# Second product of both MLPs: all four sums of weight parts of the last quarter's granules come from DRAM

## Chip, cores and metric

The kernel runs on one core of one Trainium2 chip. The metric is the device time of one execution in microseconds (us); beside it stands one execution taken by the hardware profiler, with a record of every instruction.

## What is computed

The reference runs two transformer blocks on a sequence of 512 tokens with 1024 channels, in float32. Each ends in an MLP with 4096 hidden channels; the rest (mixers, attention, norms) is not touched by the change.

```python
def squared_relu_mlp(h, w1, w2):
    return jnp.square(jax.nn.relu(h @ w1)) @ w2
# first block
x = x + squared_relu_mlp(rmsnorm(x, norm_ffn[l]), ffn_w1[l], ffn_w2[l])
# second block
u = rmsnorm_2(x, norm_mlp_g[i]) @ w_up[i]
x = x + jnp.square(jax.nn.relu(u)) @ w_down[i]
```

## The kernel before

**Number format.** To keep float32 accuracy, every operand is split into a high part (a rounding copy on ACT, `nc.scalar.copy`) and a low part (a subtraction on DVE), and a product is three matmuls: high by high, high by low, low by high (`mm3`, L275 to L277).

**The MLP.** `ffn` (from L967) runs over four quarters `q` of the hidden channels. In each, four granules of the first product (`proj_fm`, weights by `wgran`) give 1024 hidden channels, which are squared and laid down as the operand of the second product (`st_fill`). Then four granules of the second product (`st_gemm`) add 256 output channels each into the residual `x`. Granules of the second product are counted 4q + g, 0 to 15. In the last quarter (granules 12 to 15) `post` runs behind each granule: it starts the norm of the next stage on the two finished tiles of `x` (`norm_tile` in the second MLP, `ev` of `between` in the first), with work on ACT (L307, L314, L317) and on DVE (L308, L318).

**The second product** is cut into two by two blocks in Strassen's manner (Winograd's variant), with seven products instead of eight. Of each granule's weights the four blocks a11, a12, a21, a22 lie in DRAM, 256 KB each. The products need a11, a12, a22 and four sums: s1 = a21 + a22, s2 = a11 + s1, s3 = a11 + a21, s4 = a12 + s2. `st_gemm` runs the products in the order a11, a12, s2, s1, s3, s4, a22, twelve matmuls each, into three PSUM banks X, Y, Z. Behind each one a DVE addition (L947) adds the bank to `x`; X and Z then go on accumulating, so the next product into the same bank waits for that addition.

**Where the sums come from.** s1 and s2 are made in DRAM, in the scratch tile `sums`, by transfers alone: a copy of a block (issued on ACT's queue, L218) and an accumulating transfer on top (on POOL's queue, L222). `sum_jobs` (L208) writes a list of such jobs for both MLPs: for each granule copy a21, add a22 (that is s1), copy a11, add s1 (that is s2), staggered so that an add comes after its copy has had time. `job` takes `rate` jobs off the list each time it is called: in `wgran` (where `wx` is None), in `ffn` behind each granule of the first product, and in `st_gemm`. The rate is 1, but 2 from L514 to the start of the first MLP. `st_weights` (from L892) takes further jobs if the sums of its granule are not made yet (`made`). The copies are ordered behind the last weight cast of `wload` on ACT.

**Loading.** `st_weights` loads A = (a11, a12), B = (a21, s2) and C = (s1, a22) from DRAM on SP's queue (L911) into raw buffers, splits them (L304 on ACT, L305 on DVE), and makes s3 and s4 itself: one DVE addition A + B in place (L924, 128 partitions by 1024), then a split of the result. Raw buffers, and pairs of high and low buffers, go round in rings of five (`wtiles`), in two pools, "wr"/"wh"/"wl" and "wrx"/"whx"/"wlx".

**Order.** The framework lays down the order on each engine when the kernel is built, by the order in the program and its own estimate of what is ready; on the chip each engine works through its queue in that order.

Of the kernel before, what the change touches and what calls it, by code (L numbers as in the profile page):

```python
# [9 lines left out]
F32 = mybir.dt.float32  # L10
# [8 lines left out]
P = 128  # L19
KT = 8  # L20
T = 512
# [44 lines left out]
class Kern:  # L66
    def __init__(self, tc, ctx, D, out, dbg=None):
        self.tc, self.nc, self.ctx, self.D, self.out = tc, tc.nc, ctx, D, out
        self.dbg = dbg or {}
        self.const = ctx.enter_context(tc.tile_pool(name="const", bufs=1))  # L70
        self.wp = ctx.enter_context(tc.tile_pool(name="wp", bufs=3))
        self.wx, self.wn = None, 0
        self.perm = list(range(13))
        self.dp = ctx.enter_context(tc.tile_pool(name="dr", bufs=1, space=DRAM))
        self.sums = {n: [self.dp.tile([P, 2, T], F32, tag=f"{n}{g}", name=f"sums_{n}_{g}") for g in range(16)]
                     for n in ("ffn_w2", "w_down_2")}
        self.jobs, self.made, self.rate, self.rn = [], {}, 1, 0
        self.sp = ctx.enter_context(tc.tile_pool(name="sp", bufs=1))
        self.tp = ctx.enter_context(tc.tile_pool(name="tp", bufs=2))
        self.pd = ctx.enter_context(tc.tile_pool(name="pd", bufs=3, space=PSUM))  # L80
        self.ps = ctx.enter_context(tc.tile_pool(name="ps", bufs=1, space=PSUM))
        self.n = 0
# [20 lines left out]
    def psc(self, tag, bufs=None):  # L103
        return self.pc.tile([P, T], F32, tag=tag, name=self.uid(tag), bufs=bufs)
# [103 lines left out]
    def sum_jobs(self, name):  # L208


        nc, n = self.nc, 16
        W, S = self.D[name], self.sums[name]
        self.made[name] = 0

        def copy(i, j, k):
            if 0 <= i < n:
                with self.tc.issue_after(self.last_cast.ins):
                    nc.scalar.dma_start(S[i][:, j:j + 1], W[i][:, k:k + 1])  # L218

        def add(i, j, src):  # L220
            if 0 <= i < n:
                nc.gpsimd.dma_start(S[i][:, j:j + 1], src(i), accum_op=ALU.add)  # L222
                self.made[name] += j

        for i in range(n + 2):
            self.jobs += [lambda i=i: copy(i, 0, 2), lambda i=i: add(i - 1, 0, lambda g: W[g][:, 3:4]),
                          lambda i=i: copy(i, 1, 0), lambda i=i: add(i - 2, 1, lambda g: S[g][:, 0:1])]

    def job(self):
        for _ in range(self.rate):  # L230
# [327 lines left out]
    def dn_head(self, h, q, k, v, pr, gate, yb_h, yb_l):  # L558
# [125 lines left out]
        for b in range(NB):  # L684
            nc.tensor.matmul(psA[64:128, b * P:b * P + 64], M[0:64, b, 64:128], Tt[0:64, b, 0:64], start=True, stop=True)
        A = b4("dA" + e, 1)
        nc.scalar.copy(A[64:128, :, 0:64], v4(psA)[64:128, :, 0:64])
        psV = psc()
        for b in range(NB):
            nc.tensor.matmul(psV[0:64, b * P:b * P + 64], A[64:128, b, 0:64], Vt[64:128, b, 64:128], start=True, stop=True)  # L690
        TT(out=Vt[0:64, :, 64:128], in0=Vt[0:64, :, 64:128], in1=v4(psV)[0:64, :, 0:64], op=ALU.subtract)
# [200 lines left out]
    def st_weights(self, name, g):  # L892

        nc = self.nc
        while self.made[name] <= g:
            self.jobs.pop(0)()
        a, s = self.D[name][g], self.sums[name][g]
        out = []

        def parts_of(raw):  # L900
            rn = self.rn
            _, hi, lo = self.wtiles(2, T)
            self.rn = rn
            return raw, hi(), lo()

        def load(*srcs):
            raw, hi, lo = (f() for f in self.wtiles(2, T))
            j = 0
            for src in srcs:
                m = src.shape[1]  # L910
                nc.sync.dma_start(raw[:, j:j + m], src)  # L911
                j += m
            return raw, hi, lo

        def split(raw, hi, lo, c=slice(0, 2)):
            self.split_sb(hi[:, c], lo[:, c], raw[:, c])
            return [(hi[:, i], lo[:, i]) for i in range(c.start, c.stop)]

        A = load(a[:, 0:2])
        a11, a12 = split(*A)  # L920
        B = load(a[:, 2:3], s[:, 1:2])
        s2, = split(*B, slice(1, 2))
        C = load(s[:, 0:1], a[:, 3:4])
        nc.vector.tensor_tensor(out=A[0], in0=A[0], in1=B[0], op=ALU.add)  # L924
        s1, a22 = split(*C)
        s3, s4 = split(*parts_of(A[0]))
        return a11, a12, s2, s1, s3, s4, a22
# [512 lines left out]
def body(tc, D, out, dbg=None):  # L1440
    with ExitStack() as ctx:
        K = Kern(tc, ctx, D, out, dbg)
        K.setup()
        mem = K.mixer()
        with tc.tile_pool(name="sp2", bufs=1) as K.sp2:
            op = K.w_out1()
            op = K.xattn(*op, mem)
        K.rate = 1
        with tc.tile_pool(name="fp", bufs=1) as K.fp:
            K.sp2 = K.wx = K.fp  # L1450
            ev, fin = K.between()
            K.ffn("ffn_w1", "ffn_w2", *op, (0, 1, 4, 7, 8, 9, 10), ev)
            K.wx = None
            op2 = fin()
        K.perm = [2, 3, 5, 6, 0, 1, 4, 7, 8]
        mh, ml = K.mixer2(*op2)
        K.perm = list(range(13))
        xh, xl = K.pair((0, 1)), K.pair((4, 7))
        acc = K.new_acc()

        def ev(o, ps):
            K.nc.vector.scalar_tensor_tensor(out=K.x[:, o], in0=ps, scalar=0.5, in1=K.x[:, o], op0=ALU.mult, op1=ALU.add)
            K.norm_tile(o, xh, xl, acc, "norm_mlp_g_2")

        for g in range(4):
            K.proj_fm(K.wgran("w_out_2", g), mh, ml, (2 * g, 2 * g + 1), ev)
        K.dump("x5", K.x)
        with tc.tile_pool(name="fp", bufs=1) as K.fp:
            K.sp2 = K.wx = K.fp
            ev, ple = K.tail()  # L1470
            K.ffn("w_up_2", "w_down_2", xh, xl, acc, (2, 3, 5, 6, 8, 9, 10), ev)
            ple()
# [81 lines left out]
```

## Time and profile before

| | |
|---|---|
| time, median of 3 runs | 1712.49 us (1706.7 to 1714.46) |
| the profiled execution's own time | 1707.82 us |
| its span in the trace | 1706.0 us |
| PE, busy | 1681.1 us (99%) |
| DVE, busy | 1216.6 us (71%) |
| ACT, busy | 822.0 us (48%) |
| POOL, busy | 66.3 us (4%) |
| granted TensorE clock, mean | 0.996 of full |

PE is TensorE's matmul row, PEld its weight loads (which overlap), DVE VectorE, ACT ScalarE, POOL GpSimd; SP issues the loads. A name with q (ACTq, SPq) is an engine's queue, where transfers are issued. Matmuls are pipelined: one takes 0.28 us and the next starts 0.12 us after it. "L924" is line 924 of the kernel. Behind an arrow stands what ended a wait.

### The profile page before, as it was taken

Reading aid. Unit: us, or ns where it says so; the run is one execution under the profiler, and the core shown is the slowest. Engines: PE = TensorE matmul, PEld = TensorE weight load, DVE = VectorE, ACT = ScalarE, POOL = GpSimd, SP = SyncE. Lnnn points to the kernel's source line nnn. Section 1 sums busy time; section 2 is a strip of 40 time slices with the busy share of each in tenths; the row PEclk is TensorE's granted clock in tenths of the full one; section 3 lists DMA queues with packets and bytes.
Section 4 is the critical chain, followed back from the end, with each engine's and each line's share of the span. In section 5 each row is a group of like instructions: output and inputs, shape, how many; then the busy total and the mean of one; then the engine's idle time right before and its main releaser. Section 6 shows DMA issues by size and latency. Waiting matters only on the chain.

```text
span 1706.0 us, 25979 instructions
## 1 busy us (share of the span) xinstructions
PE 1681.1 (99%) x9924; PEld 1456.4 (85%) x9924; DVE 1216.6 (71%) x2574; ACT 822.0 (48%) x1462; POOL 66.3 (4%) x86
## 2 busy tenths in 40 slices
PE   9999999999999999999999999999999999999998
PEld 8988898877898989888988887788888989898987
DVE  6988885756686868688845569865556767676875
ACT  5355654544444444454444457654244444444553
POOL 0200001000000000000000000000000000000000
PEclk9999999999999999999999999999999999999999
DMA  6321357436546464423333332334464454643331
GB/s 202 100 75 53 104 162 182 112 93 171 122 134 165 131 167 131 130 93 107 100 91 101 99 87 68 93 87 118 116 188 128 132 166 131 166 131 123 100 111 50
DMA packets 81948, 205.64 MB, mean 121 GB/s; under 512 B 13088, under 2 KB 14240, under 8 KB 81824
## 3 DMA queue, kind: packets, MB, share of 16 engines
q1 hardware_dynamic: 62672, 169.29, 31.9%
q0 software_dynamic: 9216, 16.78, 6.9%
q10 hardware_dynamic: 9936, 17.91, 3.8%
q8 instruction: 78, 1.28, 0.3%
q14 instruction: 46, 0.38, 0.1%
HBM read 201.59 MB, written 35.65 MB: 139 GB/s over the span
## 4 chain that ended last, share of the span: by engine, by line
PE 88%; DVE 7%; ACT 2%; issue 1%; DMA 1%; SPq 0%; ACTq 0%; DVEq 0%
PE psd L276 21%; PE psd L275 21%; PE psd L277 21%; PE x L275 5%; PE x L276 5%; PE x L277 5%; DVE wl L257 1%; PE c L578 1%; PE c L631 1%; PE lg L1308 1%; PE po L1335 1%; ACT wh L256 1%; DVE acc L318 1%; DVE S L418 1%; PE m L1229 1%
## 5 line engine op out<-in xcount | busy, mean ns | idle before, releaser
L277 PE MATMUL psd<-S,wl 128*128 128x512 f32 (+1 forms) x1256 | 485.1, 387 | 0.6 <-DVE wl L257 0.5
L275 PE MATMUL psd<-S,wh 128*128 128x512 f32 (+1 forms) x1256 | 484.3, 386 | 0.8 <-ACT S L307 0.8
L276 PE MATMUL psd<-S,wh 128*128 128x512 f32 (+1 forms) x1192 | 459.6, 386 | 0.2
L275 PEld LDWEIGHTS psd<-S,wh 128*128 128x128 f32 x1256 | 237.2, 189 | 46.2 <-ACT S L307 1.0
L277 PEld LDWEIGHTS psd<-S,wl 128*128 128x128 f32 x1256 | 237.2, 189 | 45.8 <-DVE wl L257 1.4
L257 DVE TENSOR_TENSOR wl<-wr,wh 128x1024 fp32r<-128x1024 f32 (+2 forms) x160 | 192.0, 1200 | 107.6 <-ACT wh L256 107.0
L276 PEld LDWEIGHTS psd<-S,wh 128*128 128x128 f32 x1192 | 225.0, 189 | 43.4 <-DVE S L305 1.4
L256 ACT CAST wh<-wr 128x1024 fp32r<-128x1024 f32 (+2 forms) x160 | 164.0, 1026 | 160.3 <-PE psd L276 112.3
L276 PE MATMUL psd<-wl,S 128*128 128x256 f32 (+2 forms) x480 | 135.6, 283 | 0.3 <-DVE wl L257 0.3
L275 PE MATMUL psd<-wh,S 128*128 128x256 f32 (+2 forms) x480 | 135.5, 283 | 0.0
L277 PE MATMUL psd<-wh,S 128*128 128x256 f32 (+2 forms) x480 | 135.2, 282 | 0.0
L275 PE MATMUL x<-S,wh 128*128 128x256 f32 x452 | 128.0, 285 | 3.1 <-DVE x_fm L947 2.9
L276 PE MATMUL x<-S,wh 128*128 128x256 f32 x452 | 126.5, 281 | 0.0
L277 PE MATMUL x<-S,wl 128*128 128x256 f32 x452 | 126.0, 280 | 0.0
L276 PE MATMUL psd<-S,whx 128*128 128x512 f32 (+1 forms) x296 | 108.9, 368 | 0.1
L275 PE MATMUL psd<-S,whx 128*128 128x512 f32 (+1 forms) x296 | 107.9, 366 | 0.0
L277 PE MATMUL psd<-S,wlx 128*128 128x512 f32 (+1 forms) x296 | 107.2, 362 | 0.0
L947 DVE TENSOR_TENSOR x_fm<-x_fm,x 128x256 f32<-128x256 f32 x192 | 78.8, 417 | 27.3 <-PE x L277 27.1
L276 PEld LDWEIGHTS psd<-wl,S 128*128 128x128 f32 x480 | 90.4, 188 | 1.0 <-DVE wl L257 0.5
L275 PEld LDWEIGHTS psd<-wh,S 128*128 128x128 f32 x480 | 90.3, 188 | 0.4
L277 PEld LDWEIGHTS psd<-wh,S 128*128 128x128 f32 x480 | 90.5, 188 | 0.0
L275 PEld LDWEIGHTS x<-S,wh 128*128 128x128 f32 x452 | 84.9, 188 | 6.1 <-DVE x_fm L947 2.9
(465 smaller groups left out, 3180.4 us busy)
## 6 DMA issues: line engine op xcount, KB each, us to landing
wrx<-in_ffn_w_dram SPq DMA_DIRECT2D x32, 512.0 KB
wrx<-in_w_up_dram SPq DMA_DIRECT2D x20, 512.0 KB
wr<-in_w_in_qk_dram SPq DMA_DIRECT2D x16, 512.0 KB
sums_ffn_w<-in_ffn_w_dram ACTq DMA_DIRECT2D x32, 256.0 KB
wr<-in_ffn_w_dram SPq DMA_DIRECT2D x16, 512.0 KB
sums_w_down<-in_w_down_dram ACTq DMA_DIRECT2D x32, 256.0 KB
wr<-in_w_in_v_dram SPq DMA_DIRECT2D x12, 512.0 KB
wr<-in_w_up_dram SPq DMA_DIRECT2D x12, 512.0 KB
```

What stands on the lines that cost most here:

```text
L256: self.last_cast = nc.scalar.copy(hi[:, c], raw[:, c])
L257: nc.vector.tensor_tensor(out=lo[:, c], in0=raw[:, c], in1=hi[:, c].bitcast(F32), op=ALU.subtract)
L275: mm(ps, ah, bh, start=first, stop=False, skip_group_check=more)
L276: mm(ps, ah, bl, start=False, stop=False, skip_group_check=more)
L277: self.last_mm = mm(ps, al, bh, start=False, stop=last, skip_group_check=more)
L318: nc.vector.tensor_tensor(out=acc, in0=acc, in1=sq, op=ALU.add)
L418: nc.vector.tensor_scalar(out=d, in0=d, scalar1=ag[:, j, 0:1], scalar2=r[:, j:j + 1], op0=ALU.subtract, op1=ALU.mult)
L578: nc.tensor.matmul(blk(ps, b), lhs(b), rhs(b), start=True, stop=True)
L631: nc.tensor.matmul(ps[:, b * n:(b + 1) * n], lhs[:, b], rhs(b), start=True, stop=True)
L947: TT(out=x[n][t], in0=x[n][t], in1=ps, op=op)
L1229: nc.tensor.matmul(pX[:, :W], PT[:, tt], va[:, tt], start=True, stop=True)
L1308: nc.tensor.matmul(ps[:, i, K0:], qs[:, 2 * e2 + i, cs], kd[:, w, kc], start=(w == 0), stop=(w == 1))
```

## The change

In granules 12 to 15 of both MLPs s3 and s4 are made in DRAM too. `sums` gets four places there; `sum_jobs` gets, for each of them, two more copies (a11 and a12) and two more adds (a21 onto the first, s2 onto the second), and a granule counts as made with its last add. Within an entry of the list the add now stands ahead of the copy. `st_weights` loads (a11, a12), (s1, s2), (s3, s4) and a22 alone, and splits each; the addition L924 is not run for these granules. The rate of jobs is 2 in both MLPs.

```diff
-        self.sums = {n: [self.dp.tile([P, 2, T], F32, tag=f"{n}{g}", name=f"sums_{n}_{g}") for g in range(16)]
+        self.sums = {n: [self.dp.tile([P, 2 if g < 12 else 4, T], F32, tag=f"{n}{g}", name=f"sums_{n}_{g}") for g in range(16)]
                      for n in ("ffn_w2", "w_down_2")}
...
         def add(i, j, src):
             if 0 <= i < n:
                 nc.gpsimd.dma_start(S[i][:, j:j + 1], src(i), accum_op=ALU.add)
-                self.made[name] += j
+                self.made[name] += j == (1 if i < 12 else 3)
 
         for i in range(n + 2):
-            self.jobs += [lambda i=i: copy(i, 0, 2), lambda i=i: add(i - 1, 0, lambda g: W[g][:, 3:4]),
-                          lambda i=i: copy(i, 1, 0), lambda i=i: add(i - 2, 1, lambda g: S[g][:, 0:1])]
+            self.jobs += [lambda i=i: add(i - 1, 0, lambda g: W[g][:, 3:4]), lambda i=i: copy(i, 0, 2),
+                          lambda i=i: add(i - 2, 1, lambda g: S[g][:, 0:1]), lambda i=i: copy(i, 1, 0)]
+            if i - 2 >= 12:
+                self.jobs += [lambda i=i: copy(i - 2, 2, 0), lambda i=i: copy(i - 2, 3, 1),
+                              lambda i=i: add(i - 2, 2, lambda g: W[g][:, 2:3]), lambda i=i: add(i - 2, 3, lambda g: S[g][:, 1:2])]
...
+        if g >= 12:
+            a11, a12 = split(*load(a[:, 0:2]))
+            s1, s2 = split(*load(s[:, 0:2]))
+            s3, s4 = split(*load(s[:, 2:4]))
+            a22, = split(*load(a[:, 3:4]), slice(0, 1))
+            return a11, a12, s2, s1, s3, s4, a22
         A = load(a[:, 0:2])
...
             K.sp2 = K.wx = K.fp
+            K.rate = 2
             ev, fin = K.between()
             K.ffn("ffn_w1", "ffn_w2", *op, (0, 1, 4, 7, 8, 9, 10), ev)
-            K.wx = None
+            K.wx, K.rate = None, 1
...
             K.sp2 = K.wx = K.fp
+            K.rate = 2
             ev, ple = K.tail()
             K.ffn("w_up_2", "w_down_2", xh, xl, acc, (2, 3, 5, 6, 8, 9, 10), ev)
```

## Rows read from the trace of the kernel before

**Rows 1.** Busy times of the whole span, from the page.

```profile
PE 1681.1 (99%) x9924; PEld 1456.4 (85%) x9924; DVE 1216.6 (71%) x2574; ACT 822.0 (48%) x1462; POOL 66.3 (4%) x86
```

**Rows 2.** Busy us by stretch: PE, PEld, DVE, ACT, POOL, clock, DMA share, GB/s.

```profile
610.00:694.60 84.60, 84.51 (x527) 75.44 (x527) 61.49 (x96) 36.88 (x48) 2.44 (x3) 1.00 0.50 145
...
736.00:779.50 43.50, 41.50 (x338) 40.46 (x338) 40.11 (x69) 25.56 (x37) 0.00 (x0) 1.00 0.33 97
...
1592.00:1633.50 41.50, 40.46 (x338) 39.66 (x337) 38.19 (x65) 22.77 (x34) 0.00 (x0) 1.00 0.41 134
```

**Rows 3.** PE's waits, first and second MLP: total, times, longest.

```profile
PE x L275 <- DVE x_fm L947: 2.0, 2, 1.7
PE pss L338 <- DVE e L335: 0.8, 2, 0.6
PE pss L338 <- ACT bc L340: 0.7, 1, 0.7
...
PE x L275 <- DVE x_fm L947: 0.9, 1, 0.9
PE pss L326 <- DVE acc L318: 0.5, 1, 0.5
```

**Rows 4.** Chain of waits, last products of the first MLP: start, us, what.

```profile
754.31 0.77 DVE wr L924
...
757.90 1.20 DVE acc L318 x2
...
762.11 0.34 DVE x_fm L947
```

**Rows 5.** DVE's timeline there: start, us; in brackets idle before and releaser.

```profile
746.66 1.23 DVE L305 TENSOR_TENSOR wlx<-wrx,whx 128x1024 fp32r<-128x1024 f32 x1 [0.55 <-ACT whx L304]
...
754.23 1.22 DVE L924 TENSOR_TENSOR wr<-wr,wr 128x1024 f32<-128x1024 f32 x1
...
765.17 1.22 DVE L924 TENSOR_TENSOR wrx<-wrx,wrx 128x1024 f32<-128x1024 f32 x1
766.60 0.42 DVE L947 TENSOR_TENSOR x_fm<-x_fm,x 128x256 f32<-128x256 f32 x1 [0.21 <-PE x L277]
```

**Rows 6.** DVE's timeline, last products of the second MLP.

```profile
1613.69 1.23 DVE L305 TENSOR_TENSOR wlx<-wr,whx 128x1024 fp32r<-128x1024 f32 x1 [0.59 <-ACT whx L304]
...
1620.43 1.22 DVE L924 TENSOR_TENSOR wrx<-wrx,wrx 128x1024 f32<-128x1024 f32 x1
1621.56 0.42 DVE L947 TENSOR_TENSOR x_fm<-x_fm,x 128x256 f32<-128x256 f32 x1
```

**Rows 7.** All instructions of L924: ns min/median/max, first and last start.

```profile
L924 DVE TENSOR_TENSOR wrx<-wrx,wrx x16: 1217/1219/1222, 486.7 to 1620.4; 128x1024 f32<-128x1024 f32 x16
L924 DVE TENSOR_TENSOR wrx<-wrx,wr x8: 1217/1218/1220, 461.3 to 1573.1; 128x1024 f32<-128x1024 f32 x8
L924 DVE TENSOR_TENSOR wr<-wr,wr x8: 1217/1218/1221, 495.2 to 1609.2; 128x1024 f32<-128x1024 f32 x8
```

**Rows 8.** PE's timeline: first and last of 30 matmuls of one stretch.

```profile
775.75 0.28 PE L275 MATMUL x<-S,wh 128*128 128x256 f32 x1
...
779.19 0.29 PE L277 MATMUL x<-S,wl 128*128 128x256 f32 x1
```

**Rows 9.** Waits of SP's queue in the last products of the first MLP.

```profile
SPq L911 <- DVE wrx L924: 7.7, 1, 7.7
```

**Rows 10.** Queue table: packets, MB, share of 16 engines (q0 POOL, q10 ACT).

```profile
q0 software_dynamic: 9216, 16.78, 6.9%
q10 hardware_dynamic: 9936, 17.91, 3.8%
```

**Rows 11.** ACT's timeline around a copy's issue.

```profile
780.66 0.50 ACTq L218 DMA_DIRECT2D sums_w_down<-in_w_down_dram  x1
780.69 0.71 ACT L307 ACTIVATE S<-x_fm,g 128x512 fp32r<-128x512 f32 x1
```

## The prediction

> **What bounds the kernel now.** I began with the busy times of the page: PE works 1681.1 of 1706.0 us, so all its idle time together is 24.9 us [rows 1]. The table by stretch then shows where PE is held up. In the third quarter of the first MLP, DVE is busy 61.5 of 84.6 us and PE is never idle for long; in the second product of the last quarter DVE is busy 40.1 of 43.5 us there and 38.2 of 41.5 us in the second MLP, and PE loses time for the first time in each MLP [rows 2]. The list of what PE waited for names the place: 2.0 us in the first MLP and 0.9 us in the second on L947, the DVE addition that takes a product out of PSUM before PE may go on accumulating in that bank; behind the last granule 0.6, 0.7 and 0.5 us on the row statistics of the next norm [rows 3]. The chain of waits shows why the addition is late: before it, at 762.11, the chain runs through DVE's norm work (L308, L318) and, at 754.31, through the weight addition L924 [rows 4]. DVE works through its queue in order, and its own timeline shows how long a run without a pause is: from 746.66, where it last waited (0.55 us, for ACT), past L924 at 754.23 to the wait of PE; in the second MLP from 1613.69 past L924 at 1620.43 [rows 5, 6]. So the last quarter of each MLP is the one place where DVE, not PE, sets the pace, since only there the norm of the next stage (`post`) lies between the products.
>
> **The change, part by part.**
>
> *L924 leaves in granules 12 to 15.* One addition of 128x1024 takes 1.22 us, there are 32 of them [rows 7], and 8 go: 9.8 us of DVE. Granule 12 is prepared ahead, while PE is still in the first product, so three of four per MLP lie in the crowded stretch: 3 x 1.22 = 3.7 us. DVE's load there falls from 40.1 to 36.4 and from 38.2 to 34.5 us. PE starts a product's matmul every 0.1186 us (30 starts from 775.75 to 779.19) [rows 8], so the 4 x 84 of the four granules need 39.9 us: DVE then has 3 to 5 us to spare. What that gives is worked out wait by wait, with 1.13 us for one L924, the step from its start to that of the next instruction (1620.43 to 1621.56) [rows 6]. The long wait of the first MLP (1.7 of the 2.0 us) has one L924 in the run ahead of it; the earlier one stands before DVE's pause at 746.66 and does not count: -1.1. The short one (0.3 us) has L924 at 765.17 behind it, but after that DVE paused 0.21 us for PE at 766.60 [rows 5], so I leave it. The 0.9 us of the second MLP has one L924 in its run: all of it goes, -0.9. Together -2.0 us. The bounds: 0, if other DVE work takes the place of L924, and -2.0 -0.9 -0.6 -0.7 -0.5 = -4.7 us, if all these waits and those behind the last granule go [rows 3]. The latter I leave at nothing: PE and DVE come earlier together, and the chain behind them keeps its length.
>
> *The splits.* Seven parts are split before and after, in four instructions on ACT and four on DVE: two double, one single and one double before; three double and one single now. Nothing changes but that s3 and s4 no longer wait for an addition, and a22 comes last, as it is used last.
>
> *The loads.* Six transfers of 256 KB become three of 512 KB and one of 256 KB: 1.75 MB instead of 1.5 MB in some 10 us, and two issues fewer on SP. SP now waits for raw buffers that L924 holds, up to 7.7 us [rows 9]; that goes. There are still five raw buffers and five pairs of hi and lo. The pairs are now freed after products 1, 3, 5 and 6, so that each is refilled 8 products ahead of its use, 8 x 12 x 0.1186 = 11.4 us. That is the cover of a late load or a late cast. The rotation of the raw buffers runs one step further per granule, and the next loads fall into other buffers of the same five: nothing, under the same cover.
>
> *The sums.* Granules 12 to 15 get two more copies and two more adds each: 16 and 16 over both MLPs. The adds' queue is on POOL, which does nothing else there (66.3 us busy in all) [rows 1]; a wait of an add for its copy holds only the next adds. By the queue table the 64 adds kept the 16 DMA engines 6.9% of 1706 us, 1.84 us each; the copies 3.8% for 17.9 MB, of which 16.8 are theirs, 0.95 us each [rows 10]. The new ones cost 16 x (1.84 + 0.95) = 45 us of DMA time. The doubled rate moves others forward: in the first MLP there are 28 copies and 28 adds instead of 13 and 15, 15 x 0.95 + 13 x 1.84 = 38 us more over 338 us, 0.11 of the DMA share, where 0.50 and less is used [rows 2]. I cost it at nothing: the cover is the 11.4 us above. Without it, each call would cost what a copy and an add take, 2.8 us.
>
> *Their issue on ACT.* A copy takes ACT's queue 0.50 us, and it ran beside an ACT instruction: the next one starts 0.03 us after it [rows 11]. 15 more in the first MLP are 7.5 us if each stood alone on the path, 0 if each hides. In the crowded stretch ACT is busy 25.6 of 43.5 us [rows 2], so there is room. I take 0, by the row that shows one hidden.
>
> *Are the sums in time?* Jobs run in order of the list. 20 granule loads behind L514 at rate 2 make 40 jobs before the first MLP, which adds 32 calls x 2. Its last sum is job 88, call 24 of 32; granule 12 begins behind call 28. The other 16 are the first of the second MLP; 38 loads in the second mixer bring that list to 54, and 88 is reached in 17 calls. So no load waits for a sum. That the adds now stand ahead of the copies within a call changes nothing: a call at rate 2 holds the same pairs, and the two run on different queues.
>
> *Sum*, against the profiled execution's 1707.8 us (span 1706.0 and 1.8 around it): -1.1 - 0.9 = -2.0, so 1705.8. The median of the runs shown is 1712.5, 4.7 us above that execution; from there 1710.5.
>
> **The rivals.**
>
> *Nothing gained, 1712.5.* The order on each engine is laid down when the kernel is built, and the norm bursts alone (L308 and L318) may hold an addition as long. For it: only 0.77 us of the chain before 762 are L924's, against 1.20 us for one pair of L318 alone [rows 4]. Against it: whatever leaves a full queue moves all behind it forward.
>
> *Slower: weight splits before evictions.* s3 and s4 become ready sooner, so the planner can set a double subtraction (L305, 1.23 us) [rows 5] and a norm burst ahead of L947 in more granules than now. The price of one such place is the 1.7 us of the wait seen. The three waits of today would stay and five granules without one get it: 5 x 1.7 = 8.5 us, 1721.0. It decides from five such granules; with one or two it is 2 to 3 us and no difference. Against it: DVE's load per granule falls, so it would take bad order, not lack of time.
>
> *Slower: the new transfers delay the weights.* The queue table shows copies and adds busy on the same 16 engines as the loads [rows 10]. Were each of the four calls in the first MLP's last products to push a load past its cover by one copy and one add, that costs 4 x 2.8 = 11.2 us, 1723.7. It decides only where a load comes over 11.4 us late; the waits of PE name no DMA there [rows 3]. The Trainium skill has it as a rule, in "DMA: Bandwidth & Descriptors", section "Issuing engines are not separate DMA queues": transfers started from SP, ACT and POOL interleave on the same engines, so that a queue of one's own saves issue time alone. By that rule this rival has the mechanism; the trace agrees with the sharing and shows no wait from it.
>
> *More gained, 1707.8.* All the waits above go, 4.7 us; for it, DVE has more to spare than the waits add up to.
>
> *Not what it says, 1716.1.* If the sums of the last granules were made only when asked for, SP's queue would stand until they land: a copy and an add, 2.8 us, for the last granule of each MLP, 1710.5 + 5.6. The count of jobs speaks against it.
>
> **How the numbers follow.** Forecast 0.62, nothing gained 0.18, splits before evictions 0.08, transfers 0.04, more gained 0.06, not what it says 0.02. A measurement of this kernel can tell about 0.5%, 8.6 us, from no change. Faster by that would need a third of all PE's idle time, of which 4.7 us at most lie where the change acts: 0.06, for what I don't see and for scatter. Slower by that needs one of the two slower rivals in full, or an order shifted elsewhere: 0.10. The rest, 0.84, is the same. The range: the three shown runs lie 5.8 below to 2.0 above their median; from -4.7 to +4 of effect, with some scatter, 1702 to 1718.
>
> **What would show it.** Right: no L924 for granules 12 to 15; DVE under 37.5 us in the last products; PE's wait on L947 under 1 us over both MLPs; no PE or ACT wait on a sum or a load. Wrong: new waits of PE on L947 of 1 us and more, in more than two granules; a wait on a weight cast whose load landed late; a time below 1702 or above 1718. If the waits on L947 stay with L924 gone, the step that failed is that DVE's amount of work, not its order, makes them.

## The result and the profile after

The changed kernel takes 1717.62 us (median of 16 runs, 1711.02 to 1722.97); the kernel before, run beside it, 1707.06 us (16 runs, 1705.06 to 1714.47). The ratio of all runs is 1.0049, interval 1.0037 to 1.0061: slower by 8.4 us (the two medians alone lie 10.6 us apart), by a bit less than the 0.5% that the prediction took as its bound, but clearly not faster. Measured a second time (e12) it is 1.0037, interval 1.0018 to 1.0057. The prediction said 1710.5 from a median of 1712.5, an effect of -2.0 us; the sign is wrong. The three runs that it started from lay high: the median of sixteen is 1707.1.

The profiled execution of the changed kernel has a span of 1717.8 us, 11.8 us more than before. Its lines are numbered 3 higher in the helpers (L308 is the L305 of before, L341 the L338) and 9 higher in the product (L956 is L947, L933 is L924). The page's busy times, and the table by stretch for the last products of both MLPs (moved by the delay that has arisen by then) and for 785 to 815 us, just behind the first MLP (after PE, PEld, DVE, ACT and POOL come the granted clock, the DMA share and GB/s):

```profile
PE 1688.7 (98%) x9924; PEld 1463.8 (85%) x9924; DVE 1209.2 (70%) x2566; ACT 822.1 (48%) x1462; POOL 79.4 (5%) x102
```

```profile
741.80:785.30 43.50, 43.47 (x346) 42.06 (x346) 37.04 (x66) 25.56 (x37) 0.00 (x0) 1.00 0.38 123
1603.80:1645.30 41.50, 41.46 (x342) 40.78 (x341) 35.54 (x62) 23.29 (x34) 0.00 (x0) 1.00 0.49 164
...
785.00:815.00 30.00, 24.82 (x149) 22.42 (x148) 23.06 (x59) 11.62 (x19) 0.81 (x1) 0.89 0.32 88
```

Against [rows 2] DVE has 3.1 and 2.7 us less to do in the last products, and PE is busy there from end to end. What was meant for DVE happened. What PE waited for, behind the first MLP, in quarters 0 to 2 of the second, and in its last products:

```profile
PE pss L341 <- DVE e L338: 4.5, 1, 4.5
PE pss L341 <- ACT bc L343: 0.7, 1, 0.7
...
PE x L278 <- DVE x_fm L956: 1.9, 4, 0.8
...
PE pss L329 <- DVE acc L321: 0.4, 1, 0.4
```

Against [rows 3], the waits for the addition out of PSUM (2.0 and 0.9 us) are gone from the last products. Behind the first MLP the wait for the norm factors has grown from 0.6 to 4.5 us, and four waits stand in a stretch of the second MLP where there was none.

To see where the 11.8 us arise, the k-th matmul of PE in one trace was set beside the k-th of the other, and the distance followed from stretch to stretch (worked out from all 9924 records, in us). The stretches end at matmuls by which both kernels have done the same work, since the order on PE is not everywhere the same:

| stretch (time before) | changed | again (e12) |
|---|---|---|
| 257 to 338 us, memory and third head | +5.7 | +2.8 |
| last products of the first MLP, 736 to 781, with 9 matmuls of the next stage | -1.9 | -2.0 |
| boundary behind them, to 818 | +6.8 | +6.9 |
| second MLP, quarters 0 to 2, 1336 to 1573 | +2.3 | +2.4 |
| its last quarter, to 1641 | -1.1 | -1.1 |
| sum from 338 us to the end, rests included | +6.0 | +6.2 |

**The first row is not the change's.** Up to 410 us both kernels issue the same instructions in the same order on every engine; the difference in that stretch is one of executions. PE waits there for four transfers of 8 KB that reload a head's state (L658, before L655), in the midst of bulk loads. The chain of waits, changed kernel and kernel before (start, us, what):

```profile
264.11 4.11 DMA dY<-dV
```

```profile
264.00 3.29 DMA dY<-dV
```

After its 1.9 us of idling PE had a granted clock of half rate (1.2 GHz) for 13.65 us by the trace's clock record (in the kernel before, after 1.0 us there, none; its own stretch at half rate, 6.83 us, begins at 296 us behind another wait). In the table by stretch:

```profile
270.00:285.00 15.00, 15.00 (x77) 14.55 (x76) 4.85 (x9) 4.56 (x10) 1.61 (x2) 0.54 0.68 158
```

In the thirteen profiles of this study, all of kernels with the order of before up to there, this wait lies between nothing (e4) and 3.4 us (e6), and the stretch between 2.7 us below and 7.3 us above the kernel before's, at the ends the same two. Up to the second MLP, e6 is the kernel before with nothing changed. So the stretch is left out of the sums below; it is also the largest part of the scatter between executions that the profiles show.

**The last products of the first MLP.** The 2.0 us that PE no longer waits did not bring their end forward. Their last matmul, kernel before and changed kernel:

```profile
779.19 0.29 PE L277 MATMUL x<-S,wl 128*128 128x256 f32 x1
```

```profile
785.02 0.29 PE L280 MATMUL x<-S,wl 128*128 128x256 f32 x1
```

The distance is 5.83 us, and 5.79 us of it had arisen by 338 us. So the last products end where they ended, and what PE gained is nine wide matmuls of the second mixer's first projection: the plan puts 13 of them between the products of the last granule (776.08 to 778.85) where it had 4 (773.59 to 774.29). DVE's timeline shows what stands there instead of L924, before and then changed:

```profile
770.39 0.75 DVE L308 SCALAR_TENSOR_TENSOR S<-x_fm,g,S 128x512 fp32r<-128x512 f32 x1
...
774.47 0.75 DVE L947 TENSOR_TENSOR x_fm<-x_fm,x 128x256 f32<-128x256 f32 x2
775.13 1.22 DVE L257 TENSOR_TENSOR wl<-wr,wh 128x1024 fp32r<-128x1024 f32 x1
```

```profile
773.82 1.23 DVE L260 TENSOR_TENSOR wl<-wr,wh 128x1024 fp32r<-128x1024 f32 x1 [0.38 <-ACT wh L259]
774.96 0.75 DVE L311 SCALAR_TENSOR_TENSOR S<-x_fm,g,S 128x512 fp32r<-128x512 f32 x1
...
778.69 0.75 DVE L956 TENSOR_TENSOR x_fm<-x_fm,x 128x256 f32<-128x256 f32 x2
```

Counted from 338 us, the additions behind granule 14's norm work come 1.6 us earlier (778.69 - 5.79 = 772.90 against 774.47). But that norm work now stands one product earlier in the order: 48 narrow matmuls of PE come behind it instead of 36, 1.4 us more. And the first weight split of the next stage, which stood behind these additions, now stands ahead of the norm work and takes 1.23 us, as much as one L924. So the plan has used up the time; how the end would lie with the split back in its place, no run shows.

**The boundary.** The row sums of `tok_rs` (L329) open a chain on DVE (reciprocal square roots, L179 to L184, twice over) that ends in the copies L338, for which PE waits. The chain of waits there:

```profile
790.14 0.80 PE pss L329 x8
...
792.33 6.46 DMA wr<-in_w_in_v_dram
...
798.87 1.05 ACT wh L259
799.95 1.23 DVE wl L260
...
802.27 0.44 DVE e L338
```

The subtraction at 799.95 is a weight split of the next stage, set into the midst of the norm chain on DVE's queue. The plan of before has it at the same place of the chain, without a wait; in the changed kernel DVE stands still for it, as the two timelines show (in brackets the idle time and its releaser), before and then changed:

```profile
792.69 1.23 DVE L257 TENSOR_TENSOR wl<-wr,wh 128x1024 fp32r<-128x1024 f32 x1
```

```profile
799.95 1.23 DVE L260 TENSOR_TENSOR wl<-wr,wh 128x1024 fp32r<-128x1024 f32 x1 [2.40 <-ACT wh L259]
```

So what is new is not the place of the split but its late load: 6.46 us from issue to landing. In the kernel before, the cast of the same load starts 4.96 us after its issue (786.32 to 791.28), and with the sums held back in e3 3.6 us after it (785.61 to 789.22). An add of sums shares the DMA engines with it: issued at 790.64 on POOL, it has packets under way from 792.37 to 797.18, the load and the next one from 793.96. Before, the add's packets (786.74 to 788.62) are nearly through when the load's begin (788.34). From the first row sum to the factors at PE the chain takes 802.84 - 789.98 = 12.86 us; before, 794.99 - 783.96 = 11.03. That is 1.83 us of the 3.9 that the wait has grown.

The rest is on PE. The groups by form between the last row sum and the wait show what PE has left to do meanwhile; kernel before (786.3 to 794.9), then changed kernel (792.3 to 802.8):

```profile
L275 PE MATMUL psd<-S,wh 128*128 128x512 f32 x7 | 2.8, 407 | 0.0
L277 PE MATMUL psd<-S,wl 128*128 128x512 f32 x7 | 2.8, 394 | 0.0
L276 PE MATMUL psd<-S,wh 128*128 128x512 f32 x7 | 2.7, 391 | 0.0
```

```profile
L278 PE MATMUL psd<-S,wh 128*128 128x512 f32 x4 | 1.7, 415 | 0.0
L279 PE MATMUL psd<-S,wh 128*128 128x512 f32 x4 | 1.6, 394 | 0.0
L280 PE MATMUL psd<-S,wl 128*128 128x512 f32 x4 | 1.6, 392 | 0.0
```

21 wide matmuls of the second mixer's first projection cover the chain before, 12 after (the 24 narrow ones are the same in both). At 0.23 us from start to start the missing nine are 2.07 us. And 0.61 + 1.83 + 2.07 = 4.51 us, the wait that the trace has. The nine are those that the plan now puts between the last products. After the wait PE has half its clock for 6.83 us (the 0.89 of the stretch above); by the starts of the same matmuls that costs 2.7 us more up to 818 us (half of 6.83 would be 3.4, but PE waits in part of it). With the wait's 3.9 us and 0.2 us ahead of it these are the boundary's 6.8 us.

**The second MLP.** In quarters 0 to 2 the chain of waits now runs through loads of the second product's weights that start late:

```profile
1368.76 4.02 DMA wrx<-in_w_down_dram
...
1372.88 1.06 ACT whx L307
1373.96 1.23 DVE wlx L308
```

### The profile page after: what moved, and what is told of

Same layout as the page of the kernel before. It is cut to its first block, busy times and chain, and to the rows that moved or that the text cites. A ratio compares the mean times of both kernels' runs of the same rounds, so it can differ in the third digit from the quotient of the medians.

```text
span 1717.8 us, 26025 instructions
## 1 busy us (share of the span) xinstructions
PE 1688.7 (98%) x9924; PEld 1463.8 (85%) x9924; DVE 1209.2 (70%) x2566; ACT 822.1 (48%) x1462; POOL 79.4 (5%) x102
## 4 chain that ended last, share of the span: by engine, by line
PE 88%; DVE 6%; ACT 2%; DMA 2%; issue 1%; SPq 0%; ACTq 0%; DVEq 0%
PE psd L279 21%; PE psd L278 21%; PE psd L280 21%; PE x L278 5%; PE x L279 5%; PE x L280 5%; DVE wl L260 1%; PE c L634 1%; PE c L581 1%; PE lg L1317 1%; PE po L1344 1%; DMA wrx<-in_w_down_dram 1%; ACT wh L259 1%; DVE S L421 1%; PE m L1238 1%
## 5 line engine op out<-in xcount | busy, mean ns | idle before, releaser
L260 DVE TENSOR_TENSOR wl<-wr,wh 128x1024 fp32r<-128x1024 f32 (+2 forms) x164 | 195.7, 1193 | 110.3 <-ACT wh L259 109.8
L259 ACT CAST wh<-wr 128x1024 fp32r<-128x1024 f32 (+2 forms) x164 | 167.7, 1024 | 174.3 <-PE psd L279 118.5
L278 PE MATMUL psd<-wh,S 128*128 128x256 f32 (+2 forms) x480 | 138.3, 289 | 0.0
L280 PE MATMUL psd<-wh,S 128*128 128x256 f32 (+2 forms) x480 | 137.9, 287 | 0.0
L278 PE MATMUL x<-S,wh 128*128 128x256 f32 x460 | 129.9, 285 | 1.7 <-DVE x_fm L956 1.6
L279 PE MATMUL x<-S,wh 128*128 128x256 f32 x460 | 128.6, 281 | 0.0
L956 DVE TENSOR_TENSOR x_fm<-x_fm,x 128x256 f32<-128x256 f32 x192 | 78.7, 416 | 27.2 <-PE x L280 26.9
L278 PEld LDWEIGHTS psd<-wh,S 128*128 128x128 f32 x480 | 93.2, 194 | 0.4
L280 PEld LDWEIGHTS psd<-wh,S 128*128 128x128 f32 x480 | 93.0, 194 | 0.0
```

The source lines that it names most:

```text
L259: self.last_cast = nc.scalar.copy(hi[:, c], raw[:, c])
L260: nc.vector.tensor_tensor(out=lo[:, c], in0=raw[:, c], in1=hi[:, c].bitcast(F32), op=ALU.subtract)
L278: mm(ps, ah, bh, start=first, stop=False, skip_group_check=more)
L279: mm(ps, ah, bl, start=False, stop=False, skip_group_check=more)
L280: self.last_mm = mm(ps, al, bh, start=False, stop=last, skip_group_check=more)
L956: TT(out=x[n][t], in0=x[n][t], in1=ps, op=op)
```

## The experiments

Two theories stood first. **T**: the sums' transfers come in denser and delay weight loads, PE idles and loses its clock. **P**: the plan, the order of the instructions, has changed for the worse, with the transfers or without. The first four kernels ran beside one set of runs of the kernel before (1708.54 us), the next four beside another (1708.93), then three (1711.13) and one (1708.66). "Outside" is the sum from 338 us to the end in the profile against the kernel before, as in the table above.

**e1**, the doubled rate alone, in the kernel before:

```diff
             K.sp2 = K.wx = K.fp
+            K.rate = 2
             ev, fin = K.between()
...
-            K.wx = None
+            K.wx, K.rate = None, 1
...
             K.sp2 = K.wx = K.fp
+            K.rate = 2
             ev, ple = K.tail()
```

> The kernel before with the doubled rate of jobs in both MLPs alone: L924 and the two-sum lists stay as they were. Theory T (transfers: the sums' copies and adds, now denser, make weight loads land late, PE idles, and its clock falls behind a long wait): the waits of PE on L947 in the first two quarters of the second MLP come up as in the changed kernel (0.5 us or more there, DMA share 0.6 or more in its first quarter against 0.49 before), and the time is 2 to 6 us above before. Theory P (plan: L924's removal makes the planner lay down another order on DVE and PE behind the first MLP, and that order is what costs): the same as before within 1.5 us, and no wait above 1.5 us on the copy of the norm factors behind the first MLP.

Measured: 1708.46 us, ratio 1.0000 (0.9985 to 1.0015), outside -0.3 us. PE has no wait in quarters 0 to 2 of the second MLP, and those behind the first are as before. The doubled rate costs nothing, as the prediction had it. PE's wait for the state was 3.0 us in this profile, in a kernel that has the order of before there.

**e2**, the order within the list alone, in the kernel before:

```diff
-            self.jobs += [lambda i=i: copy(i, 0, 2), lambda i=i: add(i - 1, 0, lambda g: W[g][:, 3:4]),
-                          lambda i=i: copy(i, 1, 0), lambda i=i: add(i - 2, 1, lambda g: S[g][:, 0:1])]
+            self.jobs += [lambda i=i: add(i - 1, 0, lambda g: W[g][:, 3:4]), lambda i=i: copy(i, 0, 2),
+                          lambda i=i: add(i - 2, 1, lambda g: S[g][:, 0:1]), lambda i=i: copy(i, 1, 0)]
```

> The kernel before with the add ahead of the copy in each entry of the job list alone. Both theories: the same as before within 1 us, since a call at rate 2 holds the same pairs. If the half-rate stretch at 270 to 284 us (6.9 us of the profiled difference) came from that order, its runs would have a mean clock of 0.993 or less more often than before and be 4 to 6 us slower.

Measured: 1714.24 us, ratio 1.0020 (1.0005 to 1.0035); outside +0.9 us, all of it at the boundary, where PE waits 1.5 us for L338 instead of 0.6. Both theories missed this. The first MLP of that kernel runs at rate 1, as the second mixer does in both kernels: there one call issues one job, and whether the list begins with a copy or an add decides which of them a given call issues. As in the changed kernel an add from POOL is under way beside the load in the norm chain (packets 786.05 to 790.48), and the cast of that load starts 6.18 us after its issue instead of 4.96. The profile accounts for less than half of the 3.4 us.

**e3**, the changed kernel without jobs in the first six calls behind the first MLP:

```diff
     def job(self):
+        if self.hold:
+            self.hold -= 1
+            return
         for _ in range(self.rate):
...
-            K.wx, K.rate = None, 1
+            K.wx, K.rate, K.hold = None, 1, 6
```

> The changed kernel, with the first six calls for jobs behind the first MLP taking none, so that no copy or add of the sums runs beside the first weight loads of the second mixer. Theory T: the wait of PE on the norm factors there (4.5 us in the changed kernel) falls to 1.5 us or less, the half-rate stretch behind it goes, and the time is 4 to 6 us below the changed kernel (ratio to before about 1.002). Theory P: 3 us or more of the wait stay, as the weight subtraction still stands inside the chain of the norm on DVE and its load still shares the engines with the next load; the time is within 2 us of the changed kernel.

Measured: 1711.36 us, ratio 1.0019 (1.0002 to 1.0036), outside +2.4 us. PE's waits at the boundary:

```profile
PE pss L346 <- DVE e L343: 2.1, 1, 2.1
```

The chain is down to 10.41 us (783.23 to 793.64), shorter than before's; the cover is still 12 wide matmuls, and what is left of the wait is the nine that are missing (2.07 us). The half-rate stretch fell to 3.41 us. So T and P hold a part each of that place: the transfers lengthened the chain, the plan shortened its cover.

**e4**, the sums spread otherwise: rate 2 in the first 24 calls of the first MLP and none in its last 8 (`job` counts them down in `calls`), six calls held, rate 2 in the second mixer, rate 1 in the second MLP:

```diff
...
+            K.calls = 24
             ev, fin = K.between()
...
-            K.wx, K.rate = None, 1
+            K.wx, K.rate, K.hold, K.calls = None, 2, 6, None
...
-            K.rate = 2
+            K.rate = 1
             ev, ple = K.tail()
```

> The changed kernel with its jobs spread: rate 2 in the first three quarters of the first MLP and none in the last, none in the first six calls of the second mixer, then rate 2 there and 1 in the second MLP. Theory T: the wait behind the first MLP is 1.5 us or less, the second MLP's waits in its first two quarters go, L924's gain of 1.4 us per MLP stays, so 1 to 4 us below before. Theory P: the second MLP's waits go, but the wait behind the first MLP stays with 3 us or more; 2 to 5 us above before.

Measured: 1709.61 us, ratio 1.0007 (0.9994 to 1.0020), outside +2.8 us. The boundary is as in e3. The second MLP has its waits at rate 1 too, 2.4 us in six; so the rate is not their cause, and T falls for that place.

**e5 and e6** test what was found instead. Five raw weight buffers lie in two pools, two in one and three in the other, and a counter `rn` deals them out, one step per load (L242). Before, the first MLP steps it 80 times, and 80 mod 5 is 0; with four loads instead of three in four granules it is 84, and the second MLP starts at 4. Each quarter takes 20 loads, a multiple of 5, so the step of 4 stays all through the second MLP, and loads fall into another pool than before. e5 sets it back in the changed kernel, e6 sets it to 4 in the kernel before:

```diff
-            K.wx, K.rate = None, 1
+            K.wx, K.rate, K.rn = None, 1, 0
```

```diff
-            K.wx = None
+            K.wx, K.rn = None, 4
```

> The changed kernel with the counter that deals out the raw weight buffers set back to 0 behind the first MLP, where the kernel before also had it (80 loads, 80 mod 5 = 0; the change makes 84, so 4). Theory R (rotation): the +2.1 us that the changed kernel lost in quarters 0 to 2 of the second MLP come from loads falling into the other of the two buffer pools; they go, PE's waits on L956 in 1330 to 1590 us fall from 1.7 us to under 0.4, and the time is 1.5 to 2.5 us below the changed kernel's, ratio to before 1.0035. Theory S (density): the waits come from the doubled sums' transfers that slow the loads; nothing changes there, ratio 1.005. The boundary behind the first MLP (PE's wait for L338, 4.5 us) stays by both.

> The kernel before with that counter set to 4 behind the first MLP, and nothing else. Theory R: waits of 1.5 to 2.5 us appear in quarters 0 to 2 of the second MLP, ratio 1.001 to 1.0015. Theory S: no change, ratio 1.000.

Measured, e5: 1714.32 us, ratio 1.0026 (1.0007 to 1.0045), outside +3.2 us; e6: 1712.32 us, ratio 1.0014 (0.9997 to 1.0030), outside +5.1 us. PE's waits in 1330 to 1600 us of e5, and from 1330 to 1690 us of e6:

```profile
PE x L278 <- DVE x_fm L956: 0.2, 1, 0.2
```

```profile
PE x L275 <- DVE x_fm L947: 5.0, 6, 1.2
```

The waits go with the counter in the changed kernel, and they come with it in a kernel in which nothing else is changed (0.9 of its 5.0 us are the wait that the kernel before has in its last products). In e6 they are larger than expected: 3.8 us are lost in quarters 0 to 2 and 1.0 in the last. The interval of e6 reaches 1; what shows the cause there is the profile. The 2.3 us are the rotation's; why the other places make loads start late was not followed further.

**e7**, the change in the second MLP alone, with the list in the old order; up to the second MLP everything is as before, the counter too:

```diff
...
-                self.made[name] += j == (1 if i < 12 else 3)
+                self.made[name] += j == (3 if i >= 12 and name == "w_down_2" else 1)
...
-            if i - 2 >= 12:
+            if i - 2 >= 12 and name == "w_down_2":
...
-        if g >= 12:
+        if g >= 12 and name == "w_down_2":
...
-            K.rate = 2
             ev, fin = K.between()
```

> The change in the second MLP alone, the sums' list in the old order (copy, then add): rate 2 and the last quarter's new sums and loads only there. All that the engines do up to the second MLP is as before, the counter's phase too. The gain of its last products stands alone: -1.4 us, ratio 0.9992, if by theory R nothing else in the second MLP costs; by theory S the waits of quarters 0 to 2 come with the doubled rate, and it is +0.7 us, ratio 1.0004. Of the 1710.6-fold lottery between 260 and 305 us, whose instructions are the same in both, it has the share that the kernel before has.

(The figure ahead of "lottery" in that text is a slip and stands for nothing.) Measured: 1707.60 us, ratio 0.9984 (0.9971 to 0.9997), outside -1.4 us. PE's waits in the second MLP:

```profile
PE pss L329 <- DVE acc L321: 0.4, 1, 0.4
```

None stands on L956, and none came in its place. Of the 1.4 us outside, 1.1 are gained in the last quarter. Half of the change, on its own, does what it was to do, and this version beats both kernels.

**e8**, the changed kernel with e3's hold, e5's counter and the list's old order together:

> The changed kernel with the list's order as before, the counter set back to 0 and no sums issued in the first six calls behind the first MLP. If these three are the whole of the change's cost, both gains of 1.4 us are left and some of the boundary's wait (2.1 us were left when the six calls alone were held): ratio 0.999 to 1.000. If something else of the change costs (more instructions on SP's and POOL's queues in the first MLP, its own order of work), 1.002 or more.

Measured: 1707.12 us, ratio 0.9991 (0.9975 to 1.0007), outside -2.1 us (-2.0 last products, +1.6 boundary, -1.1 last quarter of the second MLP, the rest between them). The boundary's wait is 2.0 us, behind 12 wide matmuls. 1.0049 has become 0.9991, so the three hold the change's cost, as far as runs can tell.

**e9**, the changed kernel with the list alone in the old order (the first pair of lines of e2's diff, turned round; the extra sums stay):

> The changed kernel with copy ahead of add in the list of sums, as before the change; the extra sums stay. If the order of the list is a cost of its own (it alone gave 1.0020, interval 1.0005 to 1.0035, in the kernel before): ratio 1.002 to 1.003. If that run was chance, and the cost is what the profiles show (wait of 4.5 us at the boundary, the raw buffers' phase): 1.0045 to 1.005, with both waits in place.

Measured: 1712.31 us, ratio 1.0013 (1.0000 to 1.0027), outside +4.2 us. The boundary's wait:

```profile
PE pss L341 <- DVE e L338: 3.5, 1, 3.5
```

The chain takes 11.85 us there, 1.0 less: the add starts at 792.73, behind most of the load that was issued at 788.04, where in the changed kernel (790.64 and 792.33) it starts ahead of it. The half-rate stretch is 3.41 us instead of 6.83. The order has a price, by the profile 2 us and by the ratios 4 to 6, more than either side of the expectation allowed; what the runs show beyond the profile is open.

**e10 and e11** put the cover back: the second mixer's first projection is queued on PE behind the last product, in the changed kernel (e10) and in e8's kernel (e11):

```diff
             if h == 0:
-                self.proj_fm(self.wgran("w_in_qk2", h), xh, xl, (0, 1), ev_qk)
+                with self.tc.issue_after(self.last_mm.ins):
+                    self.proj_fm(self.wgran("w_in_qk2", h), xh, xl, (0, 1), ev_qk)
```

> The changed kernel with the second mixer's first projection queued on PE behind the last product of the first MLP. In the plan of before 21 of its wide matmuls stand between the norm sums and PE's wait for the norm factors, in that of the change 12: 9 x 0.23 = 2.1 us less work that hides the chain. Theory C (cover): with the projection back behind the products PE's wait at the boundary (4.5 us) falls to 0 to 2.2 us, and the half-rate stretch behind it goes with it; ratio 1.0015 to 1.003, the second MLP's +2.1 us stay. Theory T (transfers that delay the casts inside the chain): the chain gets longer by as much again, the wait stays above 3.5 us, ratio 1.004 or more.

> The kernel with the three repairs (old order of the list, counter set back, six calls without sums; 0.9991, 2.0 us of wait left at the boundary) and the projection queued behind the products as well. Theory C: the 2.0 us are the missing cover of 2.1 us and go; the first MLP's gain of 1.4 us and the second's are whole: ratio 0.997 to 0.9985. Against it: the 13 matmuls that the plan put ahead of the last products hid a wait there, which comes back (up to 2 us), and the ratio stays at 0.999.

Measured, e10: 1713.57 us, ratio 1.0015 (0.9998 to 1.0031), outside +2.8 us; e11: 1707.05 us, ratio 0.9988 (0.9970 to 1.0006), outside -2.1 us. The wait for L338 is gone in both, with 25 wide matmuls in the chain's cover, and in both PE waits elsewhere, once. The list of its waits from 700 to 830 us has a single line in e10, and one in e11:

```profile
PE x L278 <- DVE x_fm L956: 2.9, 1, 2.9
```

```profile
PE x L283 <- DVE x_fm L961: 2.9, 1, 2.9
```

This is the wait that the 13 matmuls hid in the changed kernel: DVE is behind at granule 15 with the next stage's weight split (1.23 us) and the norm work of granule 14, two splits and four additions of squares (L308, L318 of before), before it can take the product out. The cover is there once. The plan of before spent it behind the norm sums, that of the change between the last products, and where the chain is not delayed by transfers (e8, e11) it makes no difference which: 0.9991 and 0.9988. Of the two sides of e11's expectation it is the second that came. In e10 it does make a difference, since the 4.5 us wait and its 6.83 us at half rate are exchanged for 2.9 us and 3.41 us.

**e12**, the changed kernel once more:

> The changed kernel as it is, once more, on a chip of this call. Its parts outside the stretch from 260 to 305 us (whose instructions are those of before) add up to +5.0 us in its first profile (-1.4, +6.0, +1.8, -1.4): ratio 1.003. The first measurement gave 1.0049. If the stretch from 260 to 305 us is chance alike in both kernels: 1.002 to 1.004, PE's wait for dTb between 0.9 and 3.4 us as in the other runs, the boundary's wait 3.5 to 4.7 us, the second MLP's 1.7 to 2.5 us. If the change makes that stretch worse: 1.0045 or more and a longer wait there than 2 us.

Measured: 1714.26 us, ratio 1.0037 (1.0018 to 1.0057), outside +6.2 us. (The four parts named in that text begin and end at other places of the span than the table's.) Every wait stands where it stood:

```profile
PE pss L341 <- DVE e L338: 4.6, 1, 4.6
...
PE x L278 <- DVE x_fm L956: 2.0, 4, 1.0
```

All together, for the whole span (ratio less 1, times 1708 us) beside the profile's sum outside:

| kernel | by ratio, us | outside, us | PE on L338 at the boundary | on L947/L956, second MLP |
|---|---|---|---|---|
| before | 0 | 0 | 0.6 | 0.9 |
| changed | +8.4 | +6.0 | 4.5 | 1.9 |
| e12, again | +6.3 | +6.2 | 4.6 | 2.0 |
| e5, counter | +4.4 | +3.2 | 4.7 | 0.2 |
| e2, order in before | +3.4 | +0.9 | 1.5 | 0.9 |
| e3, hold | +3.2 | +2.4 | 2.1 | 1.9 |
| e9, old order | +2.2 | +4.2 | 3.5 | 2.4 |
| e10, cover | +2.6 | +2.8 | 0 | 2.0 |
| e6, counter in before | +2.4 | +5.1 | 0.6 | 5.0 |
| e4, spread | +1.2 | +2.8 | 2.0 | 2.4 |
| e1, rate in before | 0.0 | -0.3 | 0.6 | 0.9 |
| e8, three repairs | -1.5 | -2.1 | 2.0 | 0.3 |
| e11, and cover | -2.0 | -2.1 | 0 | 0 |
| e7, second MLP alone | -2.7 | -1.4 | 0.6 | 0 |

The two columns agree within 2.7 us, about what the intervals of the ratios allow. The 0.9 in the last column is the wait in the last products that the change removes.

## Why the prediction was wrong

**L924 in the crowded stretch: right as to DVE's work.** DVE was to have 36.4 and 34.5 us of work there; it has 37.0 and 35.5. PE's waits on L947 in the last products of both MLPs went, as the step said they would.

**Second MLP, -0.9: right.** -1.1 us in its last quarter, in the changed kernel and in e7 alike, and in e7 nothing stands against it. The prediction had taken one L924 of a run of DVE without pauses; there that way of reading [rows 6] held.

**First MLP, -1.1: failed.** The wait of 1.7 us went, but the last products end no earlier (0.04 us later in the changed kernel, 0.07 in e8). Between 736 and 818 us e11, with the cover given back, gains 0.2 us, and e8, with the chain undelayed, 0.4. What happened is the bound of 0 that the prediction named, "if other DVE work takes the place of L924": a weight split of the next stage and the norm work stand earlier, and a wait of up to 2.9 us came up a granule later, which matmuls of the next stage filled. For this MLP the rival "nothing gained" was right about the last products.

**"PE and DVE come earlier together, and the chain behind them keeps its length": the step that failed most.** It took cover and chain as fixed. The plan is laid anew when an instruction leaves: the last products end where they ended, and nine matmuls that had covered the chain moved ahead of it (2.07 us). The chain grew by 1.83 us, since a load came late for a weight split in the middle of it. Then came what the sum had no term for, half the clock for 6.83 us (2.7 us). Last products and boundary together are 4.9 us worse (-1.9 + 6.8) where 1.1 better was forecast.

**"The rotation of the raw buffers ...: nothing, under the same cover": failed.** It cost 2.3 us in the changed kernel in quarters 0 to 2 of the second MLP, and in e6 3.8 us there and 1.0 in the last quarter. The prediction looked at the granules that it changed, where the cover was there. The step in the counter stays, and its price was paid more than 500 us later, in a stretch that the change touches by the rate of jobs alone, where weight loads then started late.

**"That the adds now stand ahead of the copies within a call changes nothing": failed, in a small way.** The reason given (a call at rate 2 holds the same pairs) holds at rate 2 (e1 and the changed MLPs themselves); at rate 1, behind the MLP, it does not, and there the add met the loads of the next stage.

**The sums' transfers at double rate, nothing: right** (e1), and so was the count that no load waits for a sum. The rival "the new transfers delay the weights" had the mechanism that acted, but looked for it in the first MLP's last products, where 11.4 us of cover held; it acted behind the MLP, where a load of the next stage had no such cover: 6.46 us from issue to landing in the changed kernel, where in e8, with no sums beside it, its cast starts 3.7 us after the issue (785.24 to 788.94). This is the rule of the Trainium skill that the prediction cited, "DMA: Bandwidth & Descriptors", section "Issuing engines are not separate DMA queues": transfers of all three queues share the same engines. The prediction found no wait that came of it in the trace of before; the changed kernel has one. "A wait on a weight cast whose load landed late" was among the prediction's own signs of being wrong, and it came. The rival "weight splits before evictions" came in one place, with a split of the next stage; in the changed kernel PE had matmuls to fill the wait, and in e10 and e11, where it had none, it is the wait of 2.9 us.

A slip without consequence: before the change a granule takes five transfers, not six (A is one of 512 KB), so one issue fewer on SP, not two.

The range, 1702 to 1718, held the time by luck: its middle came from three runs whose median lay 5.4 us above that of sixteen. Moved down by that, it would end at 1712.6, below the measured 1717.6.

## What to carry to other kernels

When an instruction is taken out of a full queue, ask which waits were filled by the same movable work: the cover that hides a chain behind a stage is spent only once, and a planner that fills an earlier gap with it uncovers the later one. A change in the number of loads of a round-robin over unequal pools is a change in every loop that follows, so set the counter back to where it was, or cost the other phase there. And a change of two equal halves is worth trying by halves: here one of them alone was faster than before, and both together slower.

## What was not expected of the hardware

A wait of PE costs more than its length when the clock follows it. Behind the 4.5 us at the boundary the granted clock was at half rate for 6.83 us, in the changed kernel, in e5 and in e12 alike; behind 2.0 to 2.1 us for 3.41 us in e3 and e4, but in e8 not at all; behind the 2.9 us of e10 for 3.41 us, and behind those of e11 not at all. So after waits of 2 to 3 us it came in some of these executions and not in others, and near 4.5 us it came each time.

Four transfers of 8 KB, issued while bulk loads were under way, took 3.29 us in one execution and 4.11 us in another for the last to land, though the instructions around them stood in the same order. PE's wait on them, 1.0 to 3.4 us where it had one, was followed by up to 13.65 us at half rate, and in e3, e9 and e11 (1.6 to 2.1 us) by none.
